# Six buffers of split weights, 32 bytes longer each: a hybrid-mixer trunk layer on one core

## Chip, cores and metric

The kernel runs on one NeuronCore of a Trainium2 chip. The metric is device time in microseconds (us) of one execution. Timed alone, the kernel before took a median of 1107.8 us over three runs (1107.24 to 1108.2).

## What is computed

One layer of a decoder trunk, 512 tokens of width 1024, all in float32. The input is normalised and multiplied by one wide weight matrix `w_in` (1024 x 10512). Its columns feed four causal mixers: a gated linear recurrence (HGRN2), a matrix-memory LSTM (mLSTM), sliding-window attention and a gated DeltaNet. Each branch is projected, gated and summed, goes through one output projection and is added to the input; a squared-ReLU MLP of width 4096 follows.

```python
h = _rmsnorm(x, norm_mix_g[l])
z = jnp.einsum('btd,dn->btn', h, w_in[l])
...
proj = jnp.einsum('btnw,nwd->btnd', branches, w_branch[l])
gates = jax.nn.sigmoid(gate_pre).reshape(b, t_len, N_BRANCH, D_MODEL)
merged = jnp.sum(gates * proj, axis=2)
x = x + merged @ w_out[l]
h2 = _rmsnorm(x, norm_mlp_g[l])
x = x + jnp.square(jax.nn.relu(h2 @ w_up[l])) @ w_down[l]
```

## The kernel before

The large products are done in three passes of a rounded float type (F32R). Each operand is split into a high part and the rest, and `mm3` (line 479) multiplies high by high, high by low and low by high:

```python
def mm3(o, ah, al, bh, bl, first, last):
    mm(o, ah, bh, start=first, stop=False)
    mm(o, ah, bl, start=False, stop=False)
    mm(o, al, bh, start=False, stop=last)
```

The first operand of `mm` is stationary: it is loaded into the array by a weight load of its own (PEld in the profile). The second is streamed through it, one column after the other. In the profile a matmul reads `out<-streamed,stationary` in this kernel's order of operands, so `pf<-hT_hi,whi` streams the activations against the weights `whi`, and `pt<-whi,hT_hi` streams the weights.

Weights come from memory in pieces of 1 MB (`raw`, two buffers). For each unit of work ScalarE copies half a piece into a high part (`whi`) and VectorE subtracts it from the raw weights to get the low part (`wlo`), both in `split` (line 475, recorded as line 221 in the profile like nearly all operations of ACT, DVE and POOL). `whi` and `wlo` have three buffers each (`NW = 3`), and in every unit number i of the one goes with number i of the other. They are allocated by `wtile` (line 655), which is called from `pieces_k` (line 658) and from the `piece` inside `tok_units` (line 700). Who uses them:

- `feat_units` (line 670) and the branch projections in `merge_units` (line 1549) take slices of `whi`, `whi`, `wlo` as the stationary operand of three 512-column matmuls. They are `pf<-hT...` for the input projection, `pf<-h_...` for the MLP's first product, and `pbr` for the branches. Along `feat_units` one such slice is 128 columns, 512 bytes per partition.
- `tok_units` (line 700) streams them in 256 columns (272 in one unit that carries the gate columns): `pt`, for values, attention inputs and the output projection.
- `mlp_units` (line 1648) streams them in 512 columns for the MLP's second product: `dn<-whi,uh`, `dn<-wlo,uh`, `dn<-whi,ul`.

A planner (`_Flow.lay_out`) sets the order of all instructions from its own costs and buffer counts; the addresses of buffers don't enter it. Small matmuls of the mixers are laid between those of the projections. Three kinds are used below. `dnss` (in `dn_pre`, line 916) and `ssb` (in `head_norm`, line 835) are 512-column F32R matmuls whose stationary operands are small tables of ones, `eselr` and `onesr` (lines 507 and 508). `aov` (in `at_mix`, line 1491) is a 512-column F32R matmul between two activations.

Within a partition the pools follow one another: fixed tiles (`cp`), then `wp` with the tags `w8`, `raw`, `whi`, `wlo`, then `zp` with 37 activation buffers (`z2`), then small tiles. Two fixed tiles, `pad1` and `pad2` (lines 579 and 1741), are never read or written. The buffers of one tag have the size of the largest tile of that tag; for `whi` and `wlo` that is 4 x 272 numbers, 4352 bytes, which is 17 x 256. Where the operands begin in the program before, as byte address in a partition and its remainder modulo 256:

```
hT_hi, h2_hi       32768   0      whi 0, 1, 2   115968, 120320, 124672   0, 0, 0
hT_lo, h2_lo       49152   0      wlo 0, 1, 2   129024, 133376, 137728   0, 0, 0
w8 (brh, brl, acc) 65792   0      z2, all 37 (uh, ul, mgh, sq..., aph, avd)   0
onesr (ssb)        25248 160      eselr slices (dnss)   52 to 64 and 180 to 192
```

Of the kernel before, what the change touches and what calls it, by code (L numbers as in the profile page):

```python
# [13 lines left out]
F32R = mybir.dt.float32r  # L14
# [6 lines left out]
P = 128  # L21
# [381 lines left out]
def tile_hybrid_parallel_gated_mixers(  # L403
# [11 lines left out]
    wp = ctx.enter_context(tc.tile_pool(name="wp", bufs=2))  # L415
# [6 lines left out]
    fl = _Flow(nc, {"z2": NZ, "w8": N8, "pm": 5, "pb": 3, "raw": 2, "whi": NW, "wlo": NW, "s128": NS, "hT": 1, "hL": 1},  # L422
               {"z2": RZ, "pm": RP}, WINDOW)
# [13 lines left out]
    def nm(s):  # L437
        uid[0] += 1
        return f"{s}_{uid[0]}"
# [213 lines left out]
            units.append((grp,) + u)  # L653

    def wtile(tag, shape):
        return fl.tag(wp.tile(list(shape), F32R, tag=tag, name=nm(tag), bufs=NW), tag)

    def pieces_k(box, view, kt, cols, n=2):

        out_ = []  # L660
        for a in range(n):
            def piece(raw, a=a):
                if a == 0:
                    box["hi"], box["lo"] = wtile("whi", (P, kt, cols)), wtile("wlo", (P, kt, cols))
                s_ = slice(a * kt // n, (a + 1) * kt // n)
                split(view(raw)[:, s_, :], box["hi"][:, s_, :], box["lo"][:, s_, :])
            out_.append(piece)
        return out_
# [31 lines left out]
    def tok_units(W, c0, n256, lh, ll, evac, need=None, gates=None):  # L700


        for i in range(n256):
# [4 lines left out]
            for a in range(2):  # L708
                def piece(raw, a=a, box=box, wid=wid):
                    h_, l_ = wtile("whi", (P, 4, wid)), wtile("wlo", (P, 4, wid))  # L710
                    box[a] = (h_, l_)
                    for b in range(2):
                        split(raw[:, 4 * a + 2 * b:4 * a + 2 * b + 2, :], h_[:, 2 * b:2 * b + 2, :], l_[:, 2 * b:2 * b + 2, :])
                pieces.append(piece)
# [1038 lines left out]
NW = 3  # L1753
# [29 lines left out]
```

## Time and profile before

| what | value |
|---|---|
| median of three runs | 1107.8 us (1107.24 to 1108.2) |
| the profiled execution, its own time | 1107.01 us |
| its span, first to last instruction | 1105.2 us |
| PE busy | 1090.5 us, 99% |
| PEld (weight loads, beside PE) | 938.6 us, 85% |
| DVE, ACT, POOL busy | 687.4, 541.2, 54.8 us |
| granted TensorE clock, mean | 0.998 |
| moved by DMA | 116.44 MB |

PE is the matrix engine, PEld its weight load, DVE VectorE, ACT ScalarE. Matmuls are pipelined and each one's recorded length includes what lies under the next one, so lengths can't be added: what one matmul costs is the distance from its start to the next one's start. That distance is read from the timeline (starts in steps of 0.01 us, so over several matmuls) or from the number of matmuls in a window.

### The profile page before, as it was taken

Reading aid. Unit: us, or ns where it says so; the run is one execution under the profiler, and the core shown is the slowest. Engines: PE = TensorE matmul, PEld = TensorE weight load, DVE = VectorE, ACT = ScalarE, POOL = GpSimd, SP = SyncE. Lnnn points to the kernel's source line nnn. Section 1 sums busy time; section 2 is a strip of 40 time slices with the busy share of each in tenths; the row PEclk is TensorE's granted clock in tenths of the full one; section 3 lists DMA queues with packets and bytes.
Section 4 is the critical chain, followed back from the end, with each engine's and each line's share of the span. In section 5 each row is a group of like instructions: output and inputs, shape, how many; then the busy total and the mean of one; then the engine's idle time right before and its main releaser. Section 6 shows DMA issues by size and latency. Waiting matters only on the chain.

```text
span 1105.2 us, 15183 instructions
## 1 busy us (share of the span) xinstructions
PE 1090.5 (99%) x5855; PEld 938.6 (85%) x5855; DVE 687.4 (62%) x1420; ACT 541.2 (49%) x983; POOL 54.8 (5%) x92
## 2 busy tenths in 40 slices
PE   8999999999999999999999999999999999999998
PEld 8889877899899888788888888998888888888886
DVE  5765999757987997999588334544443324444232
ACT  5764487216763867769357323334443222443220
POOL 5000033000100000100000010000000000000000
PEclk9999999999999999999999999999999999999999
DMA  6333424513452313422232252232322323232331
GB/s 233 106 88 106 153 83 141 150 38 107 171 162 69 122 49 121 135 77 77 83 108 77 76 190 77 79 111 82 111 87 104 98 93 110 81 115 76 114 114 39
DMA packets 97527, 116.44 MB, mean 105 GB/s; under 512 B 10764, under 2 KB 75744, under 8 KB 97200
## 3 DMA queue, kind: packets, MB, share of 16 engines
q1 hardware_dynamic: 92160, 109.22, 30.8%
q0 software_dynamic: 1984, 5.61, 1.7%
q10 hardware_dynamic: 3312, 0.66, 0.3%
q8 instruction: 46, 0.75, 0.3%
q14 instruction: 25, 0.20, 0.1%
HBM read 105.49 MB, written 11.55 MB: 106 GB/s over the span
## 4 chain that ended last, share of the span: by engine, by line
PE 92%; DVE 5%; issue 1%; DMA 1%; ACT 0%; POOL 0%; DVEq 0%
PE pf L432 44%; PE dn L432 16%; PE pt L432 11%; PE pbr L432 8%; PE hg L432 1%; DVE wlo L221 1%; PE dnt L432 1%; PE alo L432 1%; PE yp L432 1%; PE up L432 1%; PE aov L432 1%; PE ho L432 1%; PE mo L432 1%; PE apt L473 1%; PE dno L432 1%
## 5 line engine op out<-in xcount | busy, mean ns | idle before, releaser
L221 DVE TENSOR_TENSOR wlo<-raw,whi 128x512 fp32r<-128x512 f32 (+1 forms) x340 | 228.6, 701 | 207.5 <-ACT whi L221 207.5
L221 ACT ACTIVATE whi<-raw 128x512 fp32r<-128x512 f32 (+1 forms) x340 | 198.6, 624 | 285.6 <-PE dn L432 121.8
L432 PE MATMUL pf<-hT_lo,whi 128*128 128x512 f32 (+1 forms) x568 | 219.1, 387 | 0.4 <-DVE hT_lo L221 0.4
L432 PE MATMUL pf<-hT_hi,whi 128*128 128x512 f32 (+1 forms) x568 | 218.8, 386 | 0.0
L432 PE MATMUL pf<-hT_hi,wlo 128*128 128x512 f32 (+1 forms) x568 | 218.0, 384 | 0.0
L432 PEld LDWEIGHTS pf<-hT_hi,wlo 128*128 128x128 f32 x568 | 107.0, 188 | 19.6 <-issue 0.6
L432 PEld LDWEIGHTS pf<-hT_hi,whi 128*128 128x128 f32 x568 | 106.9, 188 | 19.2
L432 PEld LDWEIGHTS pf<-hT_lo,whi 128*128 128x128 f32 x568 | 106.8, 188 | 19.2 <-DVE hT_lo L221 0.6
L432 PE MATMUL pf<-h_lo,whi 128*128 128x512 f32 x256 | 99.7, 389 | 0.0
L432 PE MATMUL pf<-h_hi,whi 128*128 128x512 f32 x256 | 99.6, 389 | 0.0
L432 PE MATMUL pf<-h_hi,wlo 128*128 128x512 f32 x256 | 99.6, 389 | 0.0
L432 PE MATMUL dn<-whi,ul 128*128 128x512 f32 x256 | 99.6, 389 | 0.0
L432 PE MATMUL dn<-whi,uh 128*128 128x512 f32 x256 | 99.6, 389 | 0.0
L432 PE MATMUL dn<-wlo,uh 128*128 128x512 f32 x256 | 99.6, 389 | 0.0
L221 DVE TENSOR_SCALAR ur<-pf 128x512 f32<-128x512 f32 x32 | 22.1, 691 | 71.7 <-PE pf L432 71.7
L432 PE MATMUL pt<-whi,hT_lo 128*128 128x256 f32 (+1 forms) x224 | 65.0, 290 | 0.0
L432 PE MATMUL pt<-wlo,hT_hi 128*128 128x256 f32 (+1 forms) x224 | 64.5, 288 | 0.0
L432 PE MATMUL pt<-whi,hT_hi 128*128 128x256 f32 (+1 forms) x224 | 64.3, 288 | 0.0
L432 PEld LDWEIGHTS dn<-whi,ul 128*128 128x128 f32 x256 | 48.1, 188 | 10.0
L432 PEld LDWEIGHTS pf<-h_hi,whi 128*128 128x128 f32 x256 | 48.1, 188 | 10.0
L432 PEld LDWEIGHTS dn<-whi,uh 128*128 128x128 f32 x256 | 48.1, 188 | 10.0
L432 PEld LDWEIGHTS pf<-h_hi,wlo 128*128 128x128 f32 x256 | 48.1, 188 | 9.9
(421 smaller groups left out, 1934.4 us busy)
## 6 DMA issues: line engine op xcount, KB each, us to landing
raw<-in_w_in_dram SPq DMA_DIRECT2D x41, 1024.0 KB, 5.1
raw<-in_w_up_dram SPq DMA_DIRECT2D x16, 1024.0 KB, 5.2
raw<-in_w_down_dram SPq DMA_DIRECT2D x16, 1024.0 KB, 5.0
raw<-in_w_branch_dram SPq DMA_DIRECT2D x8, 1024.0 KB, 5.0
raw<-in_w_out_dram SPq DMA_DIRECT2D x4, 1024.0 KB, 4.9
xt<-in_x_dram SPq DMA_DIRECT2D x4, 512.0 KB, 6.3
acc<-in_x_dram POOLq DMA_DIRECT2D x8, 256.0 KB, 4.5
out_dram<-acc SPq DMA_DIRECT2D x7, 256.0 KB, 2.0
```

Of the source, the lines that this page charges most:

```text
L221: flow.record(key, c, lambda: fn(*call_a, **k), outs, ins, table, dma, two="accum_out" in k)
L432: fl.record("pe", c, lambda: nc.tensor.matmul(o, lhsT, rhs, start=start, stop=stop), [o], [lhsT, rhs], two=rhs.dtype == F32)
L473: fl.record("pe", 110, lambda: nc.tensor.transpose(o, i, ident), [o], [i, ident])
```

## The change

The six buffers are allocated as tiles of 4 x 272 + 8 numbers, 4384 bytes, 32 bytes more than before, and each user gets a view of the first numbers of one in the shape that it asked for.

```diff
--- before.py
+++ after.py
@@ -653,7 +653,10 @@
             units.append((grp,) + u)
 
     def wtile(tag, shape):
-        return fl.tag(wp.tile(list(shape), F32R, tag=tag, name=nm(tag), bufs=NW), tag)
+
+        full = wp.tile([P, 4 * 272 + 8], F32R, tag=tag, name=nm(tag), bufs=NW)
+        n = shape[1] * shape[2]
+        return fl.tag(full, tag)[:, 0:n].rearrange("p (k c) -> p k c", c=shape[2])
 
     def pieces_k(box, view, kt, cols, n=2):
```

No instruction is added, removed or moved: on each of the five engines the order of instructions, their shapes and their waits are those of before. Other addresses are all that changes. In the changed program they are, with the remainder modulo 256:

```
whi 0, 1, 2   115968, 120352, 124736   0, 32, 64
wlo 0, 1, 2   129120, 133504, 137888   96, 128, 160
z2, all 37, and the small tiles behind them    192 bytes later (z2: remainder 192)
```

`hT`, `h2`, `w8`, `raw`, `onesr` and `eselr` stay where they were. Within a buffer a slice of 128 or 512 columns lies a multiple of 256 bytes from the buffer's start, so it has its buffer's remainder.

## Rows read from the trace of the kernel before

**Rows 1.** The page: the span, its engines (part 1), the chain that ended last (part 4).

```profile
span 1105.2 us, 15183 instructions
PE 1090.5 (99%) x5855; PEld 938.6 (85%) x5855; DVE 687.4 (62%) x1420; ACT 541.2 (49%) x983; POOL 54.8 (5%) x92
...
PE 92%; DVE 5%; issue 1%; DMA 1%; ACT 0%; POOL 0%; DVEq 0%
```

**Rows 2.** Waits of the two splitting engines: waiter <- releaser: total us, times, longest us.

```profile
DVE wlo L221 <- ACT whi L221: 207.5, 91, 4.2
...
ACT whi L221 <- PE dn L432: 121.8, 29, 4.3
```

**Rows 3.** Matmul groups by shape, whole span: busy us, mean ns of one, idle before.

```profile
L432 PE MATMUL pf<-hT_lo,whi 128*128 128x512 f32 x520 | 205.8, 396 | 0.0
...
L432 PE MATMUL pf<-h_lo,whi 128*128 128x512 f32 x256 | 99.7, 389 | 0.0
...
L432 PE MATMUL dn<-whi,ul 128*128 128x512 f32 x256 | 99.6, 389 | 0.0
...
L432 PE MATMUL pt<-whi,hT_lo 128*128 128x256 f32 x192 | 55.7, 291 | 0.0
...
L432 PE MATMUL pbr<-brh,whi 128*128 128x512 f32 x128 | 50.6, 395 | 0.0
...
L432 PE MATMUL pt<-wlo,mgh 128*128 128x256 f32 x128 | 36.3, 287 | 0.0
```

**Rows 4.** The same groups, from 600 us to the end alone.

```profile
L432 PE MATMUL pf<-hT_hi,whi 128*128 128x512 f32 x96 | 37.4, 390 | 0.0
...
L432 PE MATMUL pbr<-brh,whi 128*128 128x512 f32 x54 | 21.0, 389 | 0.0
```

**Rows 5.** Windows: PE, PEld, DVE, ACT, POOL busy us (count), PE clock, DMA share, GB/s.

```profile
800.00:1040.00 240.00, 240.00 (x1060) 198.79 (x1059) 93.72 (x144) 78.47 (x136) 0.00 (x0) 1.00 0.30 97
```

**Rows 6.** PE timeline, an attention matmul inserted; start us, length us, instruction.

```profile
533.11 0.39 PE L432 MATMUL aov<-aph,avd 128*128 128x512 f32 x1
...
534.70 0.39 PE L432 MATMUL aov<-apl,avd 128*128 128x512 f32 x1
534.92 0.39 PE L432 MATMUL aov<-aph,avd 128*128 128x512 f32 x1
...
535.38 0.39 PE L432 MATMUL aov<-apl,avd 128*128 128x512 f32 x1
```

**Rows 7.** PE timeline, a head-norm matmul inserted.

```profile
297.90 0.40 PE L432 MATMUL pf<-hT_hi,wlo 128*128 128x512 f32 x1
298.13 0.40 PE L432 MATMUL ssb<-sqh,onesr 128*128 128x512 f32 x1
298.37 0.39 PE L432 MATMUL pf<-hT_hi,whi 128*128 128x512 f32 x1
298.60 0.39 PE L432 MATMUL pf<-hT_lo,whi 128*128 128x512 f32 x1
```

**Rows 8.** PE timeline, first and eleventh start of a stretch with DeltaNet norm sums.

```profile
41.58 0.40 PE L432 MATMUL dnss<-sqh,eselr 128*128 128x512 f32 x1
...
43.93 0.40 PE L432 MATMUL pf<-hT_hi,whi 128*128 128x512 f32 x1
```

**Rows 9.** PE timeline, 256-column matmuls: 16 spacings alone, then six beside inserted ssb.

```profile
725.04 0.28 PE L432 MATMUL pt<-whi,mgh 128*128 128x256 f32 x1
...
726.96 0.28 PE L432 MATMUL pt<-wlo,mgh 128*128 128x256 f32 x1
...
257.53 0.28 PE L432 MATMUL pt<-whi,hT_hi 128*128 128x256 f32 x1
...
258.24 0.39 PE L432 MATMUL ssb<-sql,onesr 128*128 128x512 f32 x1
```

**Rows 10.** PE timeline, the 272-column matmuls, first start to the 97th.

```profile
89.50 0.28 PE L432 MATMUL pt<-whi,hT_hi 128*128 128x272 f32 x1
...
101.60 0.38 PE L473 MATMUL gzt<-identt,gz 128*128 128x128 f32 x2
```

## Prediction

> **What bounds the kernel now.** I read the page first. PE is busy 99% of the span and 92% of the chain that ended last is PE [rows 1]. The engine that multiplies is therefore the bound in nearly every stage, and a nanosecond more or less between two matmuls reaches the end. Weight loads are busy 85% of the span at the same time, so they must lie beside the matmuls: while one matmul streams, the next one's weights are read.
>
> Next I looked at whether the splitting engines hold PE up. VectorE's longest wait is for ScalarE's half of a split, and ScalarE waits 121.8 us in all for `dn` matmuls to give a buffer back [rows 2]. The splits run ahead of PE and stand at their own doorstep. DVE and ACT are busy 62% and 49%.
>
> Then the distance between matmuls. In the MLP 1060 matmuls of 512 columns touch a window of 240 us at a granted clock of 1.00, which is 2.4 GHz [rows 5]. Each reaches 0.39 us, so the distance is 240.39 / 1060 = 226.8 ns. At 2.4 GHz the 512 columns alone take 213.3 ns; some 13 ns come on top of each.
>
> **What the trace says of remainders.** The change alters addresses alone, so the question is whether the distance depends on them. The kernel before has three natural tests, because a few small tables don't begin at a multiple of 256.
>
> - Around `aov`, a foreign matmul that is laid between those of the projection, both operands and its weights begin at remainder 0. Ten distances take 535.38 - 533.11 = 2.27 us, 227 ns each [rows 6]. A foreign matmul as such disturbs nothing.
> - `ssb` has its stationary table at remainder 160. From the matmul during which that table is loaded, three distances take 298.60 - 297.90 = 0.70 us, 233 ns each [rows 7]. Three undisturbed ones would take 0.68 us: one visit to another remainder costs about 20 ns, spread over three matmuls.
> - `dnss` has its tables at remainders from 52 to 64. In a stretch in which they come thick, ten distances take 43.93 - 41.58 = 2.35 us, 235 ns each [rows 8], 8 ns more than in the first test.
>
> So a 512-column stream in step with weights that all have one remainder runs at its even pace, and a weight load that leaves this remainder breaks the step. After the change every triple of matmuls does so: `whi`, `whi`, `wlo` have remainders r, r, r + 96 (r = 0, 32 or 64).
>
> For shorter streams the sign differs. 256-column matmuls stand 1.92 us / 16 = 120 ns apart where nothing comes between, and 0.71 us / 6 = 118 ns apart beside inserted `ssb` [rows 9]. The one unit of 272 columns has rows of 1088 bytes, so its streamed weights already step through remainders 0, 64, 128, 192. Its 96 distances take 12.10 us, 126.0 ns each [rows 10], against (272 + 32) / 2.4 = 126.7 ns if the 13 ns were kept.
>
> **The sum.** No instruction is added, removed or moved, so there are only distances to price.
>
> 1. 512-column triples: 520 + 256 for `pf`, 128 for `pbr`, 256 for `dn`, together 1160 [rows 3]. From 600 us on, where the pace is even, lie 256 + 256 + 96 + 54 = 662 of them [rows 3, 4]. The price of a triple is bounded by 0 (if a steady alternation falls into step again) and 3 x 8.3 = 25 ns (the thick `dnss` stretch). I take 20 ns from `ssb`: its table lies an odd multiple of 32 bytes from its neighbours, as `wlo` now does from `whi`, and its disturbance lasts three matmuls, just until the next `wlo`. 662 x 20 ns = 13.2 us.
> 2. The other 498 triples lie in mixed stages. Their matmuls are 394 to 396 ns long in the mean against 389 in the MLP [rows 3]: part of them are out of step already, because of the small matmuls between. I charge half, 10 ns: 5.0 us.
> 3. For `dn` the streamed operand moves and the stationary `uh`, `ul` stand together at 192. I price it like the others, since only the distance between the two readers can matter there; it is in the 662.
> 4. 256-column matmuls with streamed weights: 3 x (192 + 128) = 960 [rows 3], at -2 to 0 ns; I take -1.7: -1.6 us. The 96 of 272 columns change nothing that counts.
> 5. Splits by ACT and DVE write to other addresses. Nothing shows a price; both engines stand waiting for PE over and over [rows 2], so a few per cent more would be covered. Without that cover each per cent of DVE's 687 us would be worth up to 7 us.
> 6. The activation buffers move by 192 bytes together. Among themselves their distances stay, so small matmuls between two of them should keep their pace: nothing.
>
> Together 13.2 + 5.0 - 1.6 = +16.6 us. The profiled execution took 1107.0 us (span 1105.2 and 1.8 around it), so about 1123.6; the median of the runs stands 0.8 above that execution. I forecast **1124 us**, slower by 1.5%.
>
> **The rivals.**
>
> *No change, 1107.8 us.* For it: a lasting alternation of remainders might settle into an even pace of its own, since what is seen in the trace is single visits. The 272-column unit alternates all the time and shows no loss. Against it: that unit is not in the 512-column regime, and `dnss` shows ten disturbed matmuls in a row. A rule of the Trainium skill would give this case too: "TensorE: Matmul & The Clock Gate", in the section on what each phase is for, says that the two operands come through independent read ports, and that loading the next weights takes nothing from the running matmul. By it no address could matter and the sum would be 0; rows 7 and 8 speak against it. Chance 0.14.
>
> *Faster, about 1099 us.* The mechanism is the opposite reading. The 13 ns over the pure stream would be a clash of two readers that begin at one remainder, and other remainders would ease it. Its place is every matmul on split weights, its price what 256 columns show, -2 ns: 3 x 1160 + 960 + 96 = 4536 matmuls give -9.1 us. For it: rows 9 and 10. Against it: for 512 columns, where most of the time is, every visit to another remainder made things longer. It decides if the distances in the MLP fall below 226.7 ns. All 13 ns would even be 59 us; no row shows such a thing. Chance 0.10.
>
> *Less slow, about 1113 us.* Only one of the three pairs, or only the stationary use, breaks the step: a third of the 18 us. It is in the forecast's range.
>
> *The change does something else.* Allocation could round buffers up and keep one remainder. The addresses of the changed program exclude that. The chance that the shift of the activation buffers matters more than the six is in the width of the range.
>
> **How the numbers follow.** Slower, in all its sizes, gets 0.76, no change 0.14, faster 0.10; 0.2% of 1107.8 is 2.2 us, about what a measurement tells from no change. The upper end: 25 ns for each of 1160 triples is 29 us, less 1.6, less what the mixed stages have already (25 x 498 / 2 = 6 us): +21 us; with some room for `dn` and the shifted activations 1132. The lower end takes in most of no change, 1106. Outside lie the faster case and a little above 1132.
>
> **What would show it.** In the changed profile a window of 240 us in the MLP should hold about 1030 matmuls rather than 1060 (240.39 / 233.3). Lengths of `pf<-h`, `dn` and `pbr` should rise above 389 ns, and the shares of the stages past 600 us should carry two thirds of the loss. Windows with 256-column matmuls should hold slightly more of them. I am wrong if the MLP still holds 1060 matmuls in such a window, or more; or if PE begins to wait for `whi` or `wlo`.

## The result, and the profile after

The changed kernel takes a median of 1118.95 us over four runs (1118.42 to 1119.51); the kernel before takes 1107.52 us beside it (four runs, 1106.78 to 1108.2). The ratio is 1.0105, with a 95% interval of 1.0093 to 1.0117: slower by 1.05%, where 1.5% was forecast. The profiled execution took 1118.42 us, 11.4 more than that of before.

The page of the kernel after, its span and engines (part 1) and its chain that ended last (part 4):

```profile
span 1116.6 us, 15183 instructions
PE 1101.6 (99%) x5855; PEld 934.9 (84%) x5855; DVE 688.2 (62%) x1420; ACT 541.6 (49%) x983; POOL 55.3 (5%) x92
...
PE 93%; DVE 5%; issue 1%; ACT 0%; DMA 0%; DVEq 0%
```

The same instructions are there, and PE's busy time has grown by 11.1 us [rows 1]. DVE's and ACT's is the same to within 1 us: what the two splitting engines write costs nothing more at the new addresses. Nor does PE wait for them: neither view of waits, before or after, has a wait of PE for `whi` or `wlo`. Their own longest waits, in the view of waits of the kernel after, are those of before with three or four us on top [rows 2]:

```profile
DVE wlo L221 <- ACT whi L221: 211.4, 91, 4.3
...
ACT whi L221 <- PE dn L432: 124.8, 29, 4.4
```

So the time went into the distances between matmuls. The groups by shape of the kernel after (busy us, mean ns of one, idle before) show it per kind:

```profile
L432 PE MATMUL pf<-hT_lo,whi 128*128 128x512 f32 x520 | 207.2, 398 | 0.0
...
L432 PE MATMUL pf<-h_lo,whi 128*128 128x512 f32 x256 | 100.7, 394 | 0.0
...
L432 PE MATMUL dn<-whi,ul 128*128 128x512 f32 x256 | 100.5, 393 | 0.0
...
L432 PE MATMUL pt<-whi,hT_lo 128*128 128x256 f32 x192 | 55.4, 289 | 0.0
...
L432 PE MATMUL pbr<-brh,whi 128*128 128x512 f32 x128 | 51.1, 400 | 0.0
...
L432 PE MATMUL pt<-wlo,mgh 128*128 128x256 f32 x128 | 36.1, 286 | 0.0
```

All kinds of 512 columns are longer, those of the MLP by 4 to 5 ns; those of 256 columns are 1 to 2 ns shorter [rows 3]. The window of the MLP that the prediction named (PE, PEld, DVE, ACT, POOL busy us with their counts, PE clock, DMA share, GB/s), of the kernel after:

```profile
800.00:1040.00 240.00, 240.00 (x1037) 194.54 (x1037) 93.74 (x144) 78.51 (x136) 0.00 (x0) 1.00 0.30 96
```

240.39 us / 1037 = 231.8 ns, where it was 226.8 [rows 5]. Starts of matmuls give it more sharply. The MLP works in two halves of 128 triples for `pf` and 128 for `dn`, so from the first `dn` to the next first `pf`, and from there to the next first `dn`, are 384 distances each. The PE timeline of the kernel before (start us, length us, instruction):

```profile
839.86 0.39 PE L432 MATMUL dn<-whi,uh 128*128 128x512 f32 x1
...
926.90 0.39 PE L432 MATMUL pf<-h_hi,whi 128*128 128x512 f32 x1
...
1013.94 0.39 PE L432 MATMUL dn<-whi,uh 128*128 128x512 f32 x1
```

and of the kernel after:

```profile
845.78 0.40 PE L432 MATMUL dn<-whi,uh 128*128 128x512 f32 x1
...
934.52 0.40 PE L432 MATMUL pf<-h_hi,whi 128*128 128x512 f32 x1
...
1023.63 0.39 PE L432 MATMUL dn<-whi,uh 128*128 128x512 f32 x1
```

Before, both stretches take 87.04 us, 226.7 ns each. After, `dn` takes 88.74 us (231.1 ns) and `pf` 89.11 us (232.1 ns). The MLP's first `pf` starts 3.9 us later than before (756.2 against 752.3 us), and from there to the last matmul it takes 7.5 us longer.

Classed by kind, from the starts in both traces, for matmuls that stand between others of their own shape (distances that hold a wait are left out):

| matmuls | count | distance before, after (ns) | change (us) |
|---|---|---|---|
| 512 columns, from 600 us on | 1977 | 226.7, 231.7 | +9.8 |
| 512 columns, before 600 us | 1286 | 228.4, 231.9 | +4.5 |
| 256 columns | 969 | 119.8, 118.2 | -1.5 |
| 128-column float32, whole span | 975 | | -2.0 |

The last line is no effect of addresses. It lies in the first 20 us, where the two profiled executions had different clocks; it is taken up at the end.

### The profile page after: what moved, and what is told of

The parts are those of the page before. It is cut to its first block, busy times and chain, and to the rows that moved or that the text cites. A ratio compares the mean times of both kernels' runs of the same rounds, so it can differ in the third digit from the quotient of the medians.

```text
span 1116.6 us, 15183 instructions
## 1 busy us (share of the span) xinstructions
PE 1101.6 (99%) x5855; PEld 934.9 (84%) x5855; DVE 688.2 (62%) x1420; ACT 541.6 (49%) x983; POOL 55.3 (5%) x92
## 4 chain that ended last, share of the span: by engine, by line
PE 93%; DVE 5%; issue 1%; ACT 0%; DMA 0%; DVEq 0%
PE pf L432 46%; PE dn L432 16%; PE pt L432 11%; PE pbr L432 8%; PE hg L432 1%; DVE wlo L221 1%; PE dnt L432 1%; PE alo L432 1%; PE yp L432 1%; PE up L432 1%; PE ho L432 1%; PE aov L432 1%; PE mo L432 1%; PE apt L473 1%; PE dno L432 1%
## 5 line engine op out<-in xcount | busy, mean ns | idle before, releaser
L221 ACT ACTIVATE whi<-raw 128x512 fp32r<-128x512 f32 (+1 forms) x340 | 198.8, 624 | 294.0 <-PE dn L432 124.8
L432 PEld LDWEIGHTS dn<-whi,ul 128*128 128x128 f32 x256 | 48.2, 188 | 11.4
L432 PEld LDWEIGHTS pf<-h_lo,whi 128*128 128x128 f32 x256 | 48.0, 188 | 11.1
L432 PEld LDWEIGHTS pf<-h_hi,whi 128*128 128x128 f32 x256 | 48.0, 188 | 11.1
```

Of the source, the lines that this page charges most:

```text
L221: flow.record(key, c, lambda: fn(*call_a, **k), outs, ins, table, dma, two="accum_out" in k)
L432: fl.record("pe", c, lambda: nc.tensor.matmul(o, lhsT, rhs, start=start, stop=stop), [o], [lhsT, rhs], two=rhs.dtype == F32)
```

## The experiments

Three theories stood against each other. **A** is the prediction's own step: a weight load that leaves the remainder of its neighbours breaks the step, so the alternation `whi`, `whi`, `wlo` costs. **B**: what counts is the difference, modulo 256, between where the weights begin that are being loaded and where the operand begins that is streamed meanwhile; a lasting difference costs as well, with no alternation at all. **C**: the loss comes from the buffers behind the six (`z2`), which moved by 192 bytes too. "Difference" below is weights being loaded minus streamed operand, modulo 256.

### Only the buffers behind the six (e1_z2_shift)

The six are as before. An unused tile of 48 numbers behind `wlo` moves `z2` to remainder 192.

```diff
+    padded = []
+
+    def pad_once(key, n):
+        if n and key not in padded:
+            padded.append(key)
+            wp.tile([P, n], F32, tag=key, name=key, bufs=1)
+
     def wtile(tag, shape):
-        return fl.tag(wp.tile(list(shape), F32R, tag=tag, name=nm(tag), bufs=NW), tag)
+        t = fl.tag(wp.tile(list(shape), F32R, tag=tag, name=nm(tag), bufs=NW), tag)
+        if tag == "wlo":
+            pad_once("padz", 48)
+        return t
```

> The six buffers as before (all at remainder 0); only what lies behind them moves by 192 bytes, as in the change. Theory A (what costs is that the remainder of the loaded or streamed weights changes from one matmul to the next): 1107.5 us, MLP window of 240 us holds 1060 matmuls. Theory B (what costs is any lasting difference between the remainders of the streamed operand and of the weights being loaded): only dn and the output projection see a difference now, dn goes from 226.7 to about 231 ns, about 1110 us. Theory C (the shift of the activation buffers is the cause): 1119 us.

Measured: 1108.16 us (ten runs), ratio 1.0012 (1.0002 to 1.0021). The PE timeline of this kernel:

```profile
839.17 0.39 PE L432 MATMUL dn<-whi,uh 128*128 128x512 f32 x1
...
927.06 0.39 PE L432 MATMUL pf<-h_hi,whi 128*128 128x512 f32 x1
...
1014.10 0.39 PE L432 MATMUL dn<-whi,uh 128*128 128x512 f32 x1
```

`dn` takes 87.89 us for 384 distances, 228.9 ns, though all weights that it streams have one remainder and all `uh` and `ul` that it loads have another; `pf` keeps its 87.04 us. So the shift behind the six is worth about a tenth of the loss when it stands alone, and C falls. A has no reason for the slower `dn`, since nothing alternates there. B has one: the difference is 192 now. But B had put `dn` at 231 ns and the time at 1110 us; 192 costs less than that.

### Only the six (e2_six_only)

The change as it is, with an unused tile of 16 numbers behind, which brings `z2` back to remainder 0.

```diff
+        full = wp.tile([P, 4 * 272 + 8], F32R, tag=tag, name=nm(tag), bufs=NW)
...
+        if tag == "wlo":
+            pad_once("padz", 16)
```

> The six remainders of the change (0, 32, 64 and 96, 128, 160), with a filler behind them so that the activation buffers are back at remainder 0. A and B: 1119 us, MLP window 1037 matmuls. C: 1107.5 us.

Measured: 1118.85 us (four runs), ratio 1.0106 (1.0091 to 1.0121), the time of the change. The PE timeline:

```profile
845.38 0.40 PE L432 MATMUL dn<-whi,uh 128*128 128x512 f32 x1
...
934.21 0.40 PE L432 MATMUL pf<-h_hi,whi 128*128 128x512 f32 x1
...
1023.32 0.40 PE L432 MATMUL dn<-whi,uh 128*128 128x512 f32 x1
```

`dn` takes 88.83 us and `pf` 89.11 us, as after the change. The six carry the whole loss.

### No alternation within a triple (e3_pairs_same)

The six keep their padding, but an unused tile of 40 numbers between the tags puts `wlo` 0, 1, 2 at the remainders of `whi` 0, 1, 2: 0, 32, 64. Within a unit nothing alternates; from unit to unit the remainder changes. `z2` lies at 96.

```diff
+        if tag == "wlo":
+            pad_once("padlo", 40)
+        full = wp.tile([P, 4 * 272 + 8], F32R, tag=tag, name=nm(tag), bufs=NW)
```

> whi and wlo of one unit share a remainder: 0 and 0, 32 and 32, 64 and 64; activation buffers at 96. A: the remainder changes once per unit instead of twice per triple, some 100 units of 512 columns at 20 ns: about 1109.5 us, first product of the MLP at 227 to 228 ns. B: two thirds of the units of the first product and the branches lose as in the change, dn too: about 1116 us, and the distance depends on the unit's remainder (226.7 ns at 0, more at 32 and 64).

Measured: 1119.28 us (four runs), ratio 1.0112 (1.0095 to 1.0129). The PE timeline:

```profile
845.00 0.39 PE L432 MATMUL dn<-whi,uh 128*128 128x512 f32 x1
...
934.69 0.39 PE L432 MATMUL pf<-h_hi,whi 128*128 128x512 f32 x1
...
1023.46 0.40 PE L432 MATMUL dn<-whi,uh 128*128 128x512 f32 x1
```

`dn` takes 89.69 us (233.6 ns), more than after the change, with nothing alternating. `pf` takes 88.77 us, and its starts sorted by unit tell why: 227.5 ns where the weights lie at 0 like the streamed `h2` (336 matmuls past 600 us), 233.2 ns at 32 (382) and 233.4 ns at 64 (333). Alternation isn't needed for the loss; A, which gave about 1109.5 us, falls as the whole cause. B, at about 1116 us, was 3 us too low. Alternation isn't free either. In the changed kernel units with `whi` at 0 and `wlo` at 96 stand at 232.6 ns after their `whi` matmuls, against 227.5 here: there a visit of one in three spoils the step, just as the prediction had it.

### All six at one other remainder (e4_all_32)

An unused tile of 8 numbers ahead of `whi`, no padding in the six: all six and `z2` begin at 32, `hT` and `h2` stay at 0.

```diff
+        if tag == "whi":
+            pad_once("padhi", 8)
```

> All six buffers and the activation buffers at remainder 32, hT and h2 still at 0. A: 1107.5 us. B: the products with stationary weights see a lasting difference of 32 and lose 5 ns per matmul, dn sees none: about 1117 us, pf at 232 ns, dn at 226.7 ns.

Measured: 1118.36 us (four runs), ratio 1.0102 (1.0087 to 1.0117): nearly the loss of the change, with a single 32-byte step and no two weight buffers apart. The PE timeline:

```profile
848.05 0.40 PE L432 MATMUL dn<-whi,uh 128*128 128x512 f32 x1
...
935.09 0.40 PE L432 MATMUL pf<-h_hi,whi 128*128 128x512 f32 x1
...
1024.69 0.39 PE L432 MATMUL dn<-whi,uh 128*128 128x512 f32 x1
```

This is the sharpest pair of stretches. `dn` streams weights at 32 and loads `uh`, `ul` at 32, and takes 87.04 us, 226.7 ns, to a hundredth of a microsecond that of before. `pf` loads the same buffers while `h2` at 0 streams, and takes 89.60 us, 233.3 ns. Both stretches use the same six buffers, written by the same splits: what counts is the two operands' places against each other. It excludes a price of the writers as well, since ScalarE and VectorE write at 32 in both stretches.

### Other differences for the first product (e5_diff_96_160, e6_diff_160_224)

e3 once more, with `hT` and `h2` moved too, by other sizes of `pad1` and `pad2`: to remainder 160 in e5 and 96 in e6. So the loaded weights differ from the streamed activations by 96, 128, 160, and by 160, 192, 224.

```diff
-    fixed([P, 48], F32, "pad1")
+    fixed([P, 24], F32, "pad1")
...
-    fixed([P, 32], F32, "pad2")
+    fixed([P, 56], F32, "pad2")
```

(e6: 72 and 8.)

> As the third experiment (pairs 0, 32, 64), with hT and h2 moved to remainder 160, so that weights minus streamed activations are 96, 128 and 160 in the three buffers. Theory B1 (any difference of remainders costs a 512-column matmul the same): pf at 232 to 234 ns in all three buffers, time 1119 to 1122 us. Theory B2 (two readers clash by where they meet, so the price depends on size and sign of the difference, and half of 256 may cost nothing): distances differ by buffer by more than 2 ns, one of them near 227 ns or below. In both, 256-column matmuls with a difference stay at 116 to 119 ns.

> The same with hT and h2 at remainder 96: weights minus streamed activations are 160, 192 and 224. B1: 232 to 234 ns in all three, 1119 to 1122 us. B2: 192 lies near the 228.9 ns that dn showed when its streamed weights stood 64 ahead of uh and ul; 224 and 160 differ from it.

Measured, one run each: 1122.72 and 1121.09 us, beside 1106.18 before. From the first `pf` of the MLP's second half to the next `dn`, in the PE timeline of e5:

```profile
937.26 0.40 PE L432 MATMUL pf<-h_hi,whi 128*128 128x512 f32 x1
...
1026.96 0.40 PE L432 MATMUL dn<-whi,uh 128*128 128x512 f32 x1
```

and of e6:

```profile
935.96 0.40 PE L432 MATMUL pf<-h_hi,whi 128*128 128x512 f32 x1
...
1025.38 0.39 PE L432 MATMUL dn<-whi,uh 128*128 128x512 f32 x1
```

e5 takes 89.70 us for 384 distances (233.6 ns) and e6 89.42 us (232.9 ns), where before it was 87.04. No difference but 0 is good for 512 columns, and 192 is the least bad. Of the two readings, neither came out whole: 96, 128, 160 and 224 cost within 1.2 ns of each other, as B1 has it (e5's time lies 0.7 us over its range), but 192 stands apart, and half of 256 costs as much as the rest. With no stretch of the MLP left at difference 0, e5 loses 16.5 us: about the sum that the prediction charged to the change.

All stretches of the traces above in which five matmuls of one width follow each other at one difference, sorted by that difference (mean distance in ns, number of matmuls in brackets; worked out from the starts, and from the addresses in the programs):

| difference | 512 columns | 256 columns (`pt`) |
|---|---|---|
| 0 | 226.7 (`dn`, 1525) | 119.7 (1559) |
| 32 | 233.2 (`pf`, 2442) | 118.1 (237) |
| 64 | 233.3 (`pf`, `dn`, 1208) | 115.4 (371) |
| 96 | 234.3 (`pf`, `dn`, 1150) | 117.8 (442) |
| 128 | 233.1 (`pf`, 578) | 119.0 (110) |
| 160 | 233.4 (`pf`, 1045) | 119.5 (102) |
| 192 | 228.9 (`dn`, 761), 231.0 (`pf`, 589) | 117.5 (414) |
| 224 | 233.3 (`pf`, 526) | 117.0 (494) |

The 231.0 ns of `pf` at 192 are the mean of two levels. In the PE timeline of e6, first and last start of two units of 24 matmuls, both with their weights in `whi` 1 and `wlo` 1 (remainder 32) and `h2` at 96:

```profile
779.27 0.39 PE L432 MATMUL pf<-h_hi,whi 128*128 128x512 f32 x1
...
784.53 0.40 PE L432 MATMUL pf<-h_hi,wlo 128*128 128x512 f32 x1
...
795.97 0.40 PE L432 MATMUL pf<-h_hi,whi 128*128 128x512 f32 x1
...
801.34 0.40 PE L432 MATMUL pf<-h_hi,wlo 128*128 128x512 f32 x1
```

The 23 distances take 5.26 us in the one and 5.37 us in the other. Of the 19 units at 192 in which nothing comes between, 8 stand at 229.0 to 229.3 ns and 11 at 233.3, none in between. So the difference doesn't settle the distance alone: with the same addresses a unit can run in either of two steady patterns. What selects the pattern no run shows.

For 512 columns 0 is best, for 256 columns it is worst, and 64 the best. That suggested a kernel faster than both, and two tests of how sharp the dependence is.

### A step of a whole period (e8_all_256)

As e4, with an unused tile of 64 numbers, 256 bytes.

```diff
+        if tag == "whi":
+            pad_once("padhi", 64)
```

> All six buffers and the activation buffers moved by 256 bytes. Theory B with remainders modulo 256: nothing changes, 1107 us, pf and dn at 226.7 ns. Rival: the period is longer than 256 bytes, or any move costs: 1117 to 1119 us.

Measured: 1107.56 us (ten runs), ratio 1.0002 (0.9993 to 1.0011). The PE timeline from the first `dn` to the next `pf`:

```profile
838.94 0.39 PE L432 MATMUL dn<-whi,uh 128*128 128x512 f32 x1
...
925.98 0.39 PE L432 MATMUL pf<-h_hi,whi 128*128 128x512 f32 x1
```

87.04 us, the stretch of before. Moving the six and all behind them by 256 bytes costs nothing, where 32 bytes cost 1%. With the table, in which every multiple of 32 but 0 costs 512 columns something, that makes 256 bytes the period among steps of 32.

### The better difference for 256 columns alone (e7_tok_192)

The kernel before, no padding. Only the 256-column tiles of `tok_units` begin 48 numbers (192 bytes) into their buffers, which have 64 numbers to spare there. Streamed weights at 192, loaded activations at 0: difference 64, for `pt` alone.

```diff
-    def wtile(tag, shape):
-        return fl.tag(wp.tile(list(shape), F32R, tag=tag, name=nm(tag), bufs=NW), tag)
+    def wtile(tag, shape, off=0):
...
+        n = shape[1] * shape[2]
+        full = wp.tile([P, off + n], F32R, tag=tag, name=nm(tag), bufs=NW)
+        return fl.tag(full, tag)[:, off:off + n].rearrange("p (k c) -> p k c", c=shape[2])
...
-                    h_, l_ = wtile("whi", (P, 4, wid)), wtile("wlo", (P, 4, wid))
+                    off = 48 if wid == 256 else 0
+                    h_, l_ = wtile("whi", (P, 4, wid), off), wtile("wlo", (P, 4, wid), off)
```

> The kernel before, with only the 256-column streamed weights of tok_units begun 192 bytes into their buffers (weights being loaded minus streamed = 64); every 512-column matmul keeps difference 0. Theory B (the price hangs on the difference, and its sign on the length of the stream): pt goes from 120 to about 115.5 ns, 960 matmuls x -4.4 ns = -4.2 us, MLP unchanged at 1060 per window: 1103.3 us. Rival R (the shorter distances of pt are taken back at the next wait, since the time is set by work between them): 1107 us.

Measured: 1103.77 us (six runs, 1103.28 to 1104.34) beside 1107.15 before (16 runs), ratio 0.997 (0.9958 to 0.9981). It is 0.3% faster than the kernel before, and so faster than both. One stretch of 82 distances of `pt`, first and last start, in the PE timeline of the kernel before:

```profile
103.51 0.36 PE L432 MATMUL pt<-wlo,hT_hi 128*128 128x256 f32 x1
...
113.43 0.28 PE L432 MATMUL pt<-whi,hT_lo 128*128 128x256 f32 x1
```

and of this one:

```profile
104.17 0.36 PE L432 MATMUL pt<-wlo,hT_hi 128*128 128x256 f32 x1
...
113.55 0.28 PE L432 MATMUL pt<-whi,hT_lo 128*128 128x256 f32 x1
```

9.92 us became 9.38 us: 121.0 and 114.4 ns a distance. Over all `pt` that stand between their like the mean fell from 119.5 to 115.3 ns (473 before 600 us) and from 119.8 to 115.8 ns (361 after), 3.5 us together. `dn` stays at 226.7 ns.

### Between the steps (e9_tok_208, e10_tok_176)

e7 with 52 and with 44 numbers instead of 48: differences 48 and 80.

```diff
-                    off = 48 if wid == 256 else 0
+                    off = 52 if wid == 256 else 0
```

> As e7 with 208 bytes: loaded minus streamed = 48. If the price varies smoothly between the measured 118.1 ns at 32 and 115.4 ns at 64, pt is at 116 to 117.5 ns and the time about 1104 us; if what counts is whole steps of 32 bytes, pt is at one of the two values.

> As e7 with 176 bytes: loaded minus streamed = 80, between the measured 115.4 ns at 64 and 117.8 ns at 96: pt at 115.5 to 117.5 ns, about 1104 us; or one of the two values if whole steps of 32 count.

Measured, one run each: 1107.6 and 1105.57 us. The same 82 distances in the PE timeline of e9:

```profile
104.87 0.37 PE L432 MATMUL pt<-wlo,hT_hi 128*128 128x256 f32 x1
...
114.72 0.29 PE L432 MATMUL pt<-whi,hT_lo 128*128 128x256 f32 x1
```

and of e10:

```profile
103.00 0.37 PE L432 MATMUL pt<-wlo,hT_hi 128*128 128x256 f32 x1
...
112.87 0.28 PE L432 MATMUL pt<-whi,hT_lo 128*128 128x256 f32 x1
```

9.85 and 9.87 us, 120 ns each: most of the gain is gone 16 bytes to either side of 64. Over all `pt` between their like it is 119.0 and 119.1 ns. Both expectations were missed. The dependence isn't a smooth valley, and a value at 48 or 80 can't be read off its neighbours at 32, 64 and 96. One rival is left: in e9 and e10 alone the streamed buffer begins at an odd multiple of 16 bytes, so a price of such a start by itself isn't told apart from one of the difference.

## Why the prediction was right in its sign, and too high in its size

**What bounds the kernel: right.** PE is still 99% busy and 93% of the chain; its busy time grew by 11.1 us, the span by 11.4.

**That the distance depends on remainders: right.** It was read off single visits (`ssb`, `dnss`) [rows 7, 8], and e4 shows it in one program with the same buffers, 226.7 against 233.3 ns.

**"A weight load that leaves this remainder breaks the step": half of the cause.** Leaving it does cost (units with `whi` at 0 in the changed kernel). But the prediction took alternation for the whole mechanism, and e3 and e4 lose as much with none. The rows read allowed both readings, since `ssb` and `dnss` leave their neighbours' remainder and differ from the streamed operand at once; I named one. Even the remark on `dn`, that only the distance between the two readers can matter there, was the better mechanism and wasn't followed for `pf`.

**The term of 20 ns a triple [step 1]: mis-sized.** From 600 us on a triple of `pf` or `pbr` lost 16 ns and one of `dn` 13 ns: 352 x 15.9 + 54 x 16.1 + 256 x 13.3 ns = 9.9 us, not 13.2. The 20 ns are what a triple loses at one steady difference other than 0 (3 x 6.6 in the table). The changed kernel doesn't hold one difference: its triples are at r, r, r + 96 against 0 or 192. In such a mix a distance isn't the table's for its own pair. Its `dn` stands at 227.1 ns in the mean after matmuls that stream `wlo` at 128 against loaded 192, difference 64, which held steadily takes 233.3; and at 233.5 where `whi` streams from 32. The table's values for its pairs would give 232.4 ns for `dn`, and 231.1 were measured. Taking one row's price as that of every triple was the error. That the sum still came within 5 us owes something to luck: the 20 ns of one visit happen to be what a steady difference costs, a case that the prediction didn't have.

**Mixed stages, half price [step 2]: right.** 10.5 ns a triple over 429 triples of like neighbours, 10 forecast. Part of the reason that was given can be seen: before the change these matmuls stand 228.4 ns apart already, not 226.7.

**`dn` priced like the others [step 3]: too high by half,** 20 ns against 13.3; the changed kernel and e2 show that with `z2` at 192 or at 0 it comes out alike once the six alternate (88.74 and 88.83 us).

**256 columns, -1.7 ns [step 4]: right,** -1.6 ns a matmul and -1.5 us in all. It was a small part of what is there to gain: at the best difference e7 finds more than 4 ns.

**Splits free, activations' shift free [steps 5, 6]: the first right,** by the busy times and e4. The second holds for small matmuls (in e1 their distances past the first 50 us changed by 0.1 us in all) but not for `dn` and `pt`: in e1 it cost the one 2.2 ns a distance and gave the other 2.

Together the terms that the traces show are +9.8 + 4.5 - 1.5 = +12.8 us. The line of 128 columns takes 2.0 off, which belongs to the clock of the first 20 us, and all other distances add 0.6: +11.4. What was named to look for came out: 1037 matmuls in the window (1030 forecast, 1060 before), lengths above 389 ns, `pt` denser. Of the loss 9.2 us, four fifths, lie past 600 us, where two thirds were forecast.

**The rivals.** *No change* fell with the first trace. A rule of the Trainium skill's "TensorE: Matmul & The Clock Gate", in the section on what each phase is for, would have given it too: the two operands come through independent read ports, and loading the next weights takes no SBUF read bandwidth from the running matmul. What the prediction drew from it, that no address could matter, doesn't hold here: e4's two stretches differ by 2.9%, where both took 87.04 us before and nothing but the starts of buffers was changed. Whether it is at the ports that the two readers meet, no run shows. *Faster* had the right picture for 256 columns and no more: difference 0 is their worst case, as it supposed, and the best case for 512. *Less slow* (1113 us) is about as far from the result as the forecast, on the other side (6.0 us under it, the forecast 5.0 over); its reading that only one of three pairs would count isn't what happened.

**What stays open.** Why a difference of 0 suits 512 columns and not 256 isn't shown: no view of the profile shows the two readers themselves. Nor is it shown what puts a unit at difference 192 into the one or the other of its two patterns, or how the prices of a mixed order come about. Steps finer than 32 bytes were tried for 256 columns only. The 272-column unit kept 124.8 to 126.4 ns a distance in all kernels; what each of its remainders does by itself was not tried.

## What to carry to other kernels

Where PE is the bound and every matmul loads its own weights, look at the start of both operands modulo 256 bytes: for 512-column F32R matmuls begin the streamed buffer and the one that weights are loaded from at the same remainder, so pad buffers in steps of 256 bytes, not of 32. For 256 columns measure other differences (64 was best of those tried here), and expect no smooth dependence. A single foreign row in a trace tells that an address matters, but not which relation does: a kernel that moves one operand and another that moves both separate the two.

## What the runs showed beyond that

That 32 bytes ahead of untouched buffers cost 1% of a kernel (e4), and 256 bytes nothing (e8), was not expected in this sharpness; nor that the same shift helps one width and hurts another, nor that 16 bytes beside the best place most of the gain is gone (e9, e10).

The other surprise is where runs of one kernel differ. Windows at the start, of the kernel before:

```profile
5.00:10.00 5.00, 2.05 (x13) 1.81 (x12) 1.53 (x7) 3.08 (x10) 4.30 (x10) 0.97 1.03 374
10.00:15.00 5.00, 4.46 (x24) 4.22 (x25) 4.93 (x12) 3.96 (x10) 0.00 (x0) 0.69 0.85 299
15.00:20.00 5.00, 5.00 (x45) 5.00 (x43) 4.24 (x12) 4.26 (x12) 0.00 (x0) 1.00 1.03 373
```

of the kernel after:

```profile
5.00:10.00 5.00, 1.64 (x16) 1.40 (x15) 2.27 (x9) 2.76 (x9) 4.76 (x10) 1.00 1.01 370
10.00:15.00 5.00, 3.60 (x27) 2.91 (x26) 5.00 (x10) 5.00 (x13) 0.00 (x0) 1.00 0.89 304
15.00:20.00 5.00, 5.00 (x45) 5.00 (x44) 4.42 (x15) 3.31 (x10) 0.07 (x1) 1.00 1.06 400
```

and of e9:

```profile
5.00:10.00 5.00, 1.58 (x15) 1.34 (x14) 2.28 (x9) 2.67 (x9) 4.77 (x10) 1.00 1.03 361
10.00:15.00 5.00, 4.19 (x22) 3.30 (x21) 5.00 (x10) 5.00 (x13) 0.00 (x0) 0.63 0.93 318
15.00:20.00 5.00, 5.00 (x33) 5.00 (x32) 4.19 (x13) 3.47 (x10) 0.00 (x0) 0.69 1.05 396
```

Between 5 and 10 us PE is busy for only 1.6 to 2.1 us of 5 while it waits for the first data. What follows differs from execution to execution: the granted clock from 10 to 15 us was 0.69 in the profiled execution of before and 1.00 in that of after; in e9 it was 0.63, and still 0.69 from 15 to 20 us. While it is low there, a distance of the first 256-column `pf` is 214 ns instead of 120 (1.2 against 2.4 GHz). That is worth one or two microseconds, whatever the addresses: it makes the line of -2.0 us in the first table, of which 0.5 us are left when the first 50 us are over, the rest being lost again in waits and other distances there. In e9 the first 50 us take 1.4 us longer than in the profiled execution of before, more than its `pt` gains (0.5 us). So the two single times of e9 and e10, 1107.6 and 1105.57 us, can't be set against each other: the granted clock of e10 was 1.00 from 5 us on. For effects below 0.2% the distances in a stretch say more than single times.
